# One of four block sums by adding DMAs, four of eight tile pairs in u and gate, and two loads placed anew

## The chip, the cores and the metric

The kernel runs on one core of a Trainium2 chip. The metric is device time in microseconds of one execution; the time before is the median of three runs. The engines are TensorE (PE; its weight loads are PEld), VectorE (DVE), ScalarE (ACT), GpSimd (POOL) and SyncE (SP). SP and POOL issue the DMAs, each from a queue worked in order; the chip's 16 DMA engines carry out what all queues issue.

## The reference

The model has two layers with a width of 2048 for 256 positions, all in fp32.

```python
def rms_norm(x, g): return x * rsqrt(mean(x * x) + EPS) * g
def gmlp_branch(xn, w_in, v_g, w_s, b_s, w_out):          # layer 0
    proj = xn @ w_in                                       # 2048 x (u 4096 | v 4096 | gate 4096)
    u, v = gelu(proj of u), rms_norm(gelu(proj of v), v_g)
    mixed = einsum('gts,bnsgc->bntgc', w_s * causal, v by chunks of 128 rows, 16 groups) + b_s
    return (u * mixed * silu(gate)) @ w_out                # 4096 x 2048
def stick_breaking_branch(xn, w_in, w_out):                # layer 1
    q, k, v, gate = split(xn @ w_in)                       # 2048 x 8192, 16 heads of 128
    a = where(mask, exp(log_sigmoid(z) + tail sums of log_sigmoid(-z)), 0)   # z = q k^T / sqrt(128)
    return ((a @ v) * silu(gate)) @ w_out                  # 2048 x 2048
for each layer: h = h + branch(rms_norm(h, norm_g[i]))
return rms_norm(h, final_g)
```

## The kernel before, in words

Every fp32 factor is split into a high part, rounded to a shorter float, and the rest: `hi` by a cast on ScalarE (L106), `lo` by a subtraction on VectorE (L108, `cut`). A product is then three matmuls, `hi*hi`, `hi*lo`, `lo*hi` (`terms`, L112 to L114), each of 128 x 128 stationary by 512 moving columns, into a PSUM bank. The weights are read from memory once and are the moving side.

A **pair** (class `Pair`) is two blocks of 512 output columns for both row tiles `t` of 128 positions, so it has four PSUM banks and 16 k-tiles. Part of the k-tiles is multiplied by Strassen's scheme in Winograd's form. The k-tiles are taken as 8 pairs (k, k + 8); `ks` of these go through the scheme, whose four weight blocks are `b11`, `b12` (first k half; first and second columns) and `b21`, `b22`. There are seven products instead of eight, called `p1`, `p5`, `p6`, `p2`, `p7`, `p3`, `p4` in their order here, each of `ks` k-tiles by three matmuls, two k-tiles to a cut. Four of them use sums of weight blocks, which VectorE makes in place (`minus`, L213): `b11 = b12 - b11` after `p1`, `b11 = b22 - b11` after `p5`, `b12 = b22 - b12` before `p7`, and `b11 = b11 - b21` before `p4`. The sums of the left side (`Left.sums`) are made once for a layer. All k-tiles outside the scheme go through `column(j)`, a raw tile of two k-tiles with 12 matmuls at a time. `ks` is 4 in the v pairs (3 pairs, and one more without the scheme at the start) and in layer 1 (`KS_A`, `KS_B`: 8 pairs for q and k, v, and gate), and 3 for the 8 pairs of u and gate (`KS_GU`). So 19 pairs use the scheme.

`head` makes `p1` and `p5` of a pair and is interleaved with `column(1)` of the pair before; `body` makes the rest. The block tiles `b11_0` to `b22_1` have one buffer each (`sraw`), raw tiles have three (`wraw`), cut tiles five (`wspl`). All weight loads are issued on SP in the order of the program's `load` calls as far as a list of dependences goes (`chain`, only until the first v pair); beyond that the order of each engine's instructions is set by a scheduler which simulates the program.

Around u and gate stands the **mixing** (L450 to L481): for each of 8 column blocks it loads the gain `vg` (L457, 256 KB) and the mixing matrices `ws` (L458, 128 KB) on POOL, masks `ws` there (`affine_select`, L459), splits it (`wh` on ScalarE L463, `wl` on VectorE L464), multiplies and makes `ym` (L480). Its loads stand inside `tc.issue_after(powers[0])`, where `powers[0]` is the first power of -0.5 on POOL (`n_r`, L94), which comes when the squares of all of x are summed. `issue_after` puts an order on instructions of the same engine as the given one. In layer 1 POOL also masks the attention weights `a` (L592), from which ScalarE makes `ah` (L704) for the product `O` (L711) on PE.

The opening works the first v pair's k-tiles as they arrive, beside the loads of x.

Of the kernel before, what the change touches and what calls it, by code (L numbers as in the profile page):

```python
# [8 lines left out]
F32 = mybir.dt.float32  # L9
F32R = mybir.dt.float32r  # L10
BF16 = mybir.dt.bfloat16
AF = mybir.ActivationFunctionType
ALU = mybir.AluOpType

P = 128
# [1 line left out]
CB = 512  # L17
WARM = 13
KS_A = 4
KS_GU = 3  # L20
KS_B = 4


# [1 line left out]
def trunk_kernel(ctx: ExitStack, tc: tile.TileContext, x, xt, gcols, wst, a_w_in, a_v_norm_g,  # L25
# [11 lines left out]
    nc = tc.nc  # L37
    PSUM = bass.MemoryType.PSUM
    NT, D = x.shape[1], x.shape[2]
    S = NT * P  # L40
# [6 lines left out]
    NV = W // CB  # L47
# [8 lines left out]
    sraw = ctx.enter_context(tc.tile_pool(name="sraw", bufs=1))  # L56
# [6 lines left out]
    half = const.tile([P, NT], F32, name="half")  # L63
# [17 lines left out]
    ssq = const.tile([P, NT, 3, NV], F32, name="ssq")  # L81

    def f(ap):
        return ap.bitcast(F32)

    powers = []

    def rstd(idx, nparts, n, name):
        tot = const.tile([P, NT], F32, name=f"{name}_tot")
        nc.vector.tensor_reduce(tot, ssq[:, :, idx, 0:nparts], axis=mybir.AxisListType.X, op=ALU.add)  # L90
        ms = const.tile([P, NT], F32, name=f"{name}_ms")
        nc.vector.tensor_scalar(ms, tot, 1.0 / n, EPS, op0=ALU.mult, op1=ALU.add)
        r = const.tile([P, NT], F32, name=f"{name}_r")
        powers.append(nc.gpsimd.tensor_tensor(r, ms, half, op=ALU.pow))  # L94
        return r

    def squares(h, c, layer, n):
# [18 lines left out]
    class Left:  # L116
# [9 lines left out]

        def sums(self, ks, out, name):

            full = []
            for i in range(2):  # L130
                sl = slice(i * ks, (i + 1) * ks)
                fl = sraw.tile([P, 4, S], F32, tag=f"b1{i + 1}_1", name=f"{name}_full{i}")
                nc.vector.tensor_add(fl[:, 0:ks], f(self.hi[:, sl, :]), f(self.lo[:, sl, :]))
                full.append(fl)
            a11, a12 = full[0][:, 0:ks, 0:P], full[1][:, 0:ks, 0:P]
            a21, a22 = full[0][:, 0:ks, P:S], full[1][:, 0:ks, P:S]
            sm = [sraw.tile([P, 2, 4, P], F32, tag=f"b2{i + 1}_1", name=f"{name}_sm{i}") for i in range(2)]
            s1, s2, s3, s4 = sm[0][:, 0, 0:ks], sm[0][:, 1, 0:ks], sm[1][:, 0, 0:ks], sm[1][:, 1, 0:ks]
            nc.vector.tensor_add(s1, a21, a22)
            nc.vector.tensor_sub(s3, a11, a21)  # L140
            nc.vector.tensor_sub(s2, s1, a11)
            nc.vector.tensor_sub(s4, a12, s2)
            for i, si in enumerate((s1, s2, s3, s4)):
                nc.scalar.copy(out[:, 0, i], si)
                nc.vector.tensor_sub(out[:, 1, i], si, f(out[:, 0, i]))
            self.s, self.ks = out, ks

        def sum_part(self, i, k):
# [19 lines left out]
    def ins_of(x):  # L168
        return x.ins if hasattr(x, "ins") else x
# [9 lines left out]
    class Pair:  # L179
# [31 lines left out]
        def minus(self, into, b0, b1):  # L211
            for g in range(len(self.groups)):
                nc.vector.tensor_sub(into[g], b0[g], b1[g])  # L213

        def head(self):
            left = self.left
            self.b11, self.b12 = self.load(0, 0), self.load(0, 1)
            self.a = self.bank("a")
            yield from self.block(self.b11, lambda k: left.part(k, 0), self.a, "p1", True)
            self.b22, self.b21 = self.load(1, 1), self.load(1, 0)  # L220
            self.minus(self.b11, self.b12, self.b11)
            self.e = self.bank("e")
            yield from self.block(self.b11, lambda k: left.sum_part(0, k), self.e, "p5", True)
            self.minus(self.b11, self.b22, self.b11)

        def body(self):
            left, off = self.left, self.left.ks
            b11, b12, b22, b21 = self.b11, self.b12, self.b22, self.b21

            def block(*args):  # L230
                for _ in self.block(*args):
                    pass
            a, e = self.a, self.e
            b = self.bank("b")
            nc.scalar.copy(b, a)
            es = jk.tile([P, CB], F32, tag="es", bufs=1, name=f"{self.name}_es")
            nc.scalar.copy(es, e)
            block(b11, lambda k: left.sum_part(1, k), b, "p6")
            c = self.bank("c")
            nc.scalar.copy(c, b)  # L240
            self.minus(b12, b22, b12)
            block(b21, lambda k: left.part(off + k, 0), a, "p2")
            nc.vector.tensor_add(b, b, es)
            block(b12, lambda k: left.sum_part(2, k), c, "p7")
            d = self.bank("d")
            nc.scalar.copy(d, c)
            self.minus(b11, b21, b11)
            block(b22, lambda k: left.sum_part(3, k), b, "p3")
            block(b11, lambda k: left.part(off + k, 1), d, "p4")
            nc.vector.tensor_add(c, c, es)  # L250
            self.banks = ((a, d), (b, c))
            if self.mid is not None:
                self.mid()
            for _ in self.column(0):
                pass
# [79 lines left out]
    def home(tag, shape, dtype, name):  # L335
        return big.tile(shape, dtype, tag=tag, name=name)
# [4 lines left out]
    left = Left(x_hi, x_lo)  # L341
# [24 lines left out]
    def split_x(k):  # L366
# [2 lines left out]
        nc.scalar.activation(x_hi[:, k, :], xk, AF.Identity, scale=g)  # L369
        nc.vector.scalar_tensor_tensor(x_lo[:, k, :], xk, g, f(x_hi[:, k, :]), op0=ALU.mult, op1=ALU.subtract)  # L370

    def evac_v(b, t, bank):
        vs = v[:, t, b * CB:(b + 1) * CB]
        nc.scalar.activation(vs, bank, AF.Gelu_apprx_tanh, scale=r1[:, t:t + 1])
        junk = jk.tile([P, CB], BF16, tag="junk", name=f"junkv{b}_{t}")
        nc.scalar.activation(junk, vs, AF.Square, accum_out=ssq[:, t, 1, b:b + 1])


    banks = [[ps_acc.tile([P, CB], F32, tag="acc", name=f"v0_acc{t}{j}") for t in range(NT)] for j in range(2)]
# [32 lines left out]
    for i in range(KD // 4):  # L412
# [32 lines left out]
    with ExitStack() as lg:  # L445
# [5 lines left out]
        def mixing(b):  # L451

            vg = pa.tile([P, CB], F32, tag="vg", name=f"vg{b}")
            ws = pb.tile([P, GPB, P], F32, tag="ws", name=f"ws{b}")

            with tc.issue_after(ins_of(powers[0])):
                nc.gpsimd.dma_start(vg, a_v_norm_g[0:1, b * CB:(b + 1) * CB].to_broadcast([P, CB]))  # L457
                nc.gpsimd.dma_start(ws, wst[:, b * GPB:(b + 1) * GPB, :])  # L458
            nc.gpsimd.affine_select(ws, ws, pattern=[[0, GPB], [1, P]], compare_op=ALU.is_ge, fill=0.0,  # L459
                                    base=0, channel_multiplier=-1)  # L460
            wh = pb.tile([P, GPB, P], F32R, tag="wh", name=f"wh{b}")
            wl = pb.tile([P, GPB, P], F32R, tag="wl", name=f"wl{b}")
            nc.scalar.copy(wh, ws)  # L463
            nc.vector.tensor_sub(wl, ws, f(wh))  # L464
            mixed[b] = []
            for t in range(NT):
                vh = pb.tile([P, CB], F32R, tag="vh", name=f"vh{b}_{t}")
                vl = pb.tile([P, CB], F32R, tag="vl", name=f"vl{b}_{t}")
                vs = v[:, t, b * CB:(b + 1) * CB]
                nc.scalar.activation(vh, vs, AF.Identity, scale=rv[:, t:t + 1])  # L470
                nc.vector.scalar_tensor_tensor(vl, vs, rv[:, t:t + 1], f(vh), op0=ALU.mult, op1=ALU.subtract)
                mp = ps_ms.tile([P, CB], F32, tag="ms", name=f"mix{b}_{t}")
                for j in range(GPB):
                    o = mp[:, j * GD:(j + 1) * GD]
                    sl = slice(j * GD, (j + 1) * GD)
                    nc.tensor.matmul(o, wh[:, j, :], vh[:, sl], start=True, stop=False)
                    nc.tensor.matmul(o, wh[:, j, :], vl[:, sl], start=False, stop=False)
                    nc.tensor.matmul(o, wl[:, j, :], vh[:, sl], start=False, stop=True)
                ym = pa.tile([P, CB], F32, tag=f"ym{t}", bufs=2, name=f"ym{b}_{t}")
                nc.vector.tensor_mul(ym, mp, vg)  # L480
                mixed[b].append(ym)  # L481
# [30 lines left out]
    with ExitStack() as lo_:  # L512
# [361 lines left out]
```

## Time and profile before

| what | value |
|---|---|
| median of three runs | 1179.2 us (1177.38 to 1179.94) |
| the profiled execution | 1180.04 us |
| its span, first to last instruction | 1178.3 us |
| mean granted clock of TensorE | 0.996 of full speed |
| busy: PE, VectorE, ScalarE, POOL | 1160.8, 945.5, 773.9, 47.7 us |
| DMA | 235.88 MB, mean 200 GB/s |
| its queues | q1 hardware_dynamic 229.67 MB, q0 software_dynamic 4.20 MB |

The span is what the trace covers; the execution's own time is 1.7 us longer. Stages of the span, roughly: v to 190 us, u and gate to 510, the first output projection to 720, q, k, v, gate and attention to 1080, then the last projection and the norm. A busy PE is not PE at its peak, as matmuls overlap: they start 0.23 us apart while one is shown as 0.39 us long. Idle time of another engine costs nothing by itself.

### The profile page before, as it was taken

The numbers are of one execution on the slowest core, as the hardware profiler recorded it, in microseconds if no ns is written. First come the engines' busy times: TensorE is split into PE (matmuls) and PEld (weight loads), VectorE is DVE, ScalarE is ACT, GpSimd is POOL, SyncE is SP. The second block draws the span as 40 slices with busy tenths as digits, with TensorE's granted clock in tenths as the row PEclk, the third lists the DMA queues.
The fourth block names the chain that finished last, engine by engine and source line by source line (L and its number), as shares of the span: only waits on it lengthen the run. The fifth ranks groups of instructions, "written<-read, shape, count | busy, mean of one in ns | idle before, by whom it ended". The sixth has DMA issues, their size and how long they took to land.

```text
span 1178.3 us, 14877 instructions
## 1 busy us (share of the span) xinstructions
PE 1160.8 (99%) x5393; PEld 961.4 (82%) x5393; DVE 945.5 (80%) x1050; ACT 773.9 (66%) x996; POOL 47.7 (4%) x55
## 2 busy tenths in 40 slices
PE   9899999999999999999999999999999999999997
PEld 6688888888888888888888887888888878888887
DVE  6889888998988987966556469999889989896564
ACT  7667577776766666765444456688679687885452
POOL 0210000110000000000000000002010000000000
PEclk9999999999999999999999999999999999999999
DMA  9875566576567576376556676466474564526772
GB/s 317 300 244 177 186 214 211 165 223 217 160 218 227 160 229 217 92 232 236 192 190 200 217 268 236 137 235 189 133 248 162 162 214 148 178 72 218 259 223 100
DMA packets 119609, 235.88 MB, mean 200 GB/s; under 512 B 7920, under 2 KB 12144, under 8 KB 119024
## 3 DMA queue, kind: packets, MB, share of 16 engines
q1 hardware_dynamic: 117648, 229.67, 59.8%
q0 software_dynamic: 1168, 4.20, 1.3%
q10 hardware_dynamic: 720, 1.07, 0.2%
q8 instruction: 42, 0.69, 0.2%
q14 instruction: 31, 0.25, 0.1%
HBM read 230.71 MB, written 4.19 MB: 199 GB/s over the span
## 4 chain that ended last, share of the span: by engine, by line
PE 77%; DVE 7%; ACT 6%; DMA 4%; issue 4%; POOL 0%; SPq 0%; POOLq 0%; DVEq 0%; ACTq 0%
PE o_acc L114 5%; PE o_acc L112 5%; PE o_acc L113 5%; PE gu_a L113 2%; PE gu_a L114 2%; PE gu_a L112 2%; PE gu_b L113 2%; PE gu_b L112 2%; PE gu_b L114 2%; PE f_acc L113 2%; PE f_acc L112 2%; PE f_acc L114 2%; PE gu_d L112 2%; PE gu_d L113 2%; PE gu_d L114 2%
## 5 line engine op out<-in xcount | busy, mean ns | idle before, releaser
L307 DVE TENSOR_TENSOR o_lo<-o_raw,o_hi 128x1024 fp32r<-128x1024 f32 x64 | 78.3, 1224 | 75.2 <-ACT o_hi L305 75.0
L305 ACT CAST o_hi<-o_raw 128x1024 fp32r<-128x1024 f32 x64 | 67.3, 1053 | 88.5 <-PE o_acc L114 62.4
L106 ACT CAST gu_hi<-gu_raw 128x1024 fp32r<-128x1024 f32 x80 | 82.9, 1052 | 62.8 <-DMA gu_raw<-in_a_w_in 45.6
L108 DVE TENSOR_TENSOR gu_lo<-gu_raw,gu_hi 128x1024 fp32r<-128x1024 f32 x80 | 96.3, 1217 | 30.2 <-ACT gu_hi L106 29.8
L106 ACT CAST gu_p_hi<-gu_b 128x1024 fp32r<-128x1024 f32 x112 | 91.5, 835 | 40.1 <-PE gu_c L114 22.6
L108 DVE TENSOR_TENSOR gu_p_lo<-gu_b,gu_p_hi 128x1024 fp32r<-128x1024 f32 x112 | 104.5, 954 | 4.6 <-ACT gu_p_hi L106 4.3
L112 PE MATMUL o_acc<-o_hi,yc 128*128 128x512 f32 x256 | 100.4, 392 | 0.0
L114 PE MATMUL o_acc<-o_hi,yc 128*128 128x512 f32 x256 | 99.8, 390 | 0.0
L113 PE MATMUL o_acc<-o_lo,yc 128*128 128x512 f32 x256 | 99.6, 389 | 0.0
L106 ACT CAST qk_p_hi<-qk_b 128x1024 fp32r<-128x1024 f32 x56 | 57.4, 1049 | 16.5 <-PE o_acc L114 6.9
L108 DVE TENSOR_TENSOR qk_p_lo<-qk_b,qk_p_hi 128x1024 fp32r<-128x1024 f32 x56 | 67.1, 1218 | 1.2 <-ACT qk_p_hi L106 1.0
L108 DVE TENSOR_TENSOR v_lo<-v_raw,v_hi 128x1024 fp32r<-128x1024 f32 x40 | 48.2, 1219 | 21.8 <-ACT v_hi L106 21.5
L106 ACT CAST v_hi<-v_raw 128x1024 fp32r<-128x1024 f32 x40 | 41.5, 1052 | 30.6 <-DMA v_raw<-in_a_w_in 22.4
L213 DVE TENSOR_TENSOR gu_b<-gu_b,gu_b 128x1024 f32<-128x1024 f32 (+1 forms) x64 | 60.2, 954 | 0.5
L307 DVE TENSOR_TENSOR f_lo<-f_raw,f_hi 128x1024 fp32r<-128x1024 f32 x28 | 34.2, 1224 | 30.1 <-ACT f_hi L305 29.9
L114 PEld LDWEIGHTS o_acc<-o_hi,yc 128*128 128x128 f32 x256 | 48.0, 188 | 10.0
L113 PEld LDWEIGHTS o_acc<-o_lo,yc 128*128 128x128 f32 x256 | 48.1, 188 | 9.8
L112 PEld LDWEIGHTS o_acc<-o_hi,yc 128*128 128x128 f32 x256 | 48.1, 188 | 9.7
L112 PE MATMUL f_acc<-f_hi,y_hi 128*128 128x512 f32 (+1 forms) x160 | 55.6, 347 | 0.0
L114 PE MATMUL f_acc<-f_hi,y_lo 128*128 128x512 f32 (+1 forms) x160 | 55.6, 347 | 0.0
L113 PE MATMUL f_acc<-f_lo,y_hi 128*128 128x512 f32 (+1 forms) x160 | 55.5, 347 | 0.0
L106 ACT CAST v_p_hi<-v_b 128x1024 fp32r<-128x1024 f32 x42 | 42.8, 1054 | 15.6 <-DVE v_b L213 14.4
(491 smaller groups left out, 3377.4 us busy)
## 6 DMA issues: line engine op xcount, KB each, us to landing
gu_raw<-in_a_w_in SPq DMA_DIRECT2D x64, 512.0 KB, 4.5
o_raw<-in_a_w_out SPq DMA_DIRECT2D x64, 512.0 KB, 4.4
v_raw<-in_a_w_in SPq DMA_DIRECT2D x39, 512.0 KB, 5.1
gu_b<-in_a_w_in SPq DMA_DIRECT2D x32, 512.0 KB, 4.8
qk_b<-in_b_w_in SPq DMA_DIRECT2D x32, 512.0 KB, 4.8
qk_raw<-in_b_w_in SPq DMA_DIRECT2D x32, 512.0 KB, 3.9
f_raw<-in_b_w_out SPq DMA_DIRECT2D x32, 512.0 KB, 4.2
v_b<-in_a_w_in SPq DMA_DIRECT2D x24, 512.0 KB, 5.6
```

What stands on the lines that cost most here:

```text
L106: nc.scalar.copy(hi[:, 0:n], raw[:, 0:n])
L108: nc.vector.tensor_sub(lo[:, 0:n], raw[:, 0:n], f(hi[:, 0:n]))
L112: nc.tensor.matmul(acc, lh, hi, start=first, stop=False, skip_group_check=True)
L113: nc.tensor.matmul(acc, lh, lo, start=False, stop=False, skip_group_check=True)
L114: nc.tensor.matmul(acc, ll, hi, start=False, stop=last, skip_group_check=True)
L213: nc.vector.tensor_sub(into[g], b0[g], b1[g])
L305: nc.scalar.copy(hi, raw)
L307: nc.vector.tensor_sub(lo, raw, f(hi))
```

## The change

- `KS_GU` goes from 3 to 4: a pair of u and gate has 4 of 8 tile pairs in the scheme, all its cuts and sums are 1024 wide, and a column has 4 raw tiles instead of 5.
- The sum `b12` with `b22` is no longer made on VectorE. A new function `plus` issues two DMAs on POOL, each reading 512 KB of `b22` from memory once more and adding it to `b12` in SBUF. Signs elsewhere change so that the sum is an addition: `b11 = b22 + b11` is a `tensor_add` now, and the left side's sums are mirrored.
- `b21` is loaded by the program after `p5` instead of with `b22`.
- The mixing loads stand inside `issue_after` of `norms[NV - 1]`, the last of the first pairs' squares of v (ScalarE), instead of `powers[0]` (POOL).
- `left.sums` works in pieces of four k-tiles; with 4 this is one piece as before.

```diff
-KS_GU = 3
+KS_GU = 4
...
-    powers = []
...
-        powers.append(nc.gpsimd.tensor_tensor(r, ms, half, op=ALU.pow))
+        nc.gpsimd.tensor_tensor(r, ms, half, op=ALU.pow)
...
-            nc.vector.tensor_add(s1, a21, a22)
-            nc.vector.tensor_sub(s3, a11, a21)
-            nc.vector.tensor_sub(s2, s1, a11)
+                nc.vector.tensor_sub(s1, a21, a22)
+                nc.vector.tensor_sub(s3, a21, a11)
+                nc.vector.tensor_sub(s2, a11, s1)
...
+        def plus(self, into, i, j):
+
+            for g, (k, n) in enumerate(self.groups):
+                nc.gpsimd.dma_start(into[g], self.src(i * self.left.ks + k, n, j), accum_op=ALU.add)
...
-            self.b22, self.b21 = self.load(1, 1), self.load(1, 0)
+            self.b22 = self.load(1, 1)
             self.minus(self.b11, self.b12, self.b11)
+            self.plus(self.b12, 1, 1)
             self.e = self.bank("e")
             yield from self.block(self.b11, lambda k: left.sum_part(0, k), self.e, "p5", True)
-            self.minus(self.b11, self.b22, self.b11)
+            self.b21 = self.load(1, 0)
+            for g in range(len(self.groups)):
+                nc.vector.tensor_add(self.b11[g], self.b22[g], self.b11[g])
...
             nc.scalar.copy(c, b)
-            self.minus(b12, b22, b12)
             block(b21, lambda k: left.part(off + k, 0), a, "p2")
...
-        nc.scalar.activation(junk, vs, AF.Square, accum_out=ssq[:, t, 1, b:b + 1])
+        norms.append(nc.scalar.activation(junk, vs, AF.Square, accum_out=ssq[:, t, 1, b:b + 1]))
...
-    left.sums(KS_A, home("xs", [P, 2, 4, KS_A, P], F32R, "xs0"), "s0")
+    left.sums(max(KS_A, KS_GU), home("xs", [P, 2, 4, max(KS_A, KS_GU), P], F32R, "xs0"), "s0")
...
-            with tc.issue_after(ins_of(powers[0])):
+            with tc.issue_after(ins_of(norms[NV - 1])):
```

Where the instructions stand now is shown at three places. The first is POOL's queue in the opening, before and then changed; `n_r` is the power, `vg` and `ws` the mixing's tiles.

```order
masks.py:197 MEMSET ident 128x128
masks.py:199 ISA
masks.py:199 AFFINE_SELECT ident<-ident 128x128
L94 TENSOR_TENSOR n_r<-n_ms,half 128x2
L457 DMA vg_1680<-in_a_v_norm_g 128x512
L458 DMA ws_1681<-in_wst 128x256
L458 DMA ws_2065<-in_wst 128x256
L459 AFFINE_SELECT ws_1681<-ws_1681 128x256
L459 AFFINE_SELECT ws_2065<-ws_2065 128x256
```

```order
masks.py:197 MEMSET ident 128x128
L467 DMA vg_1701<-in_a_v_norm_g 128x512
L468 DMA ws_1702<-in_wst 128x256
L468 DMA ws_2069<-in_wst 128x256
masks.py:199 ISA
masks.py:199 AFFINE_SELECT ident<-ident 128x128
L469 AFFINE_SELECT ws_1702<-ws_1702 128x256
L468 DMA ws_2436<-in_wst 128x256
L469 AFFINE_SELECT ws_2069<-ws_2069 128x256
```

The loads of `vg` and of the first two `ws` stood behind `n_r`; they stand ahead of the mask of `ident` now, and `n_r` comes after these rows.

The second is ScalarE's beginning, before and changed: the casts of the first raw tiles and of x, with its gain (`x_hi`).

```order
L369 ACTIVATE x_hi<-xr_127,cols 128x256
L106 CAST v_0_hi<-v_0_raw 128x1024
L369 ACTIVATE x_hi<-xr_127,cols 128x256 x3
L106 CAST v_1_hi<-v_1_raw 128x1024
L106 CAST v_2_hi<-v_2_raw 128x1024
```

```order
L377 ACTIVATE x_hi<-xr_127,cols 128x256
L104 CAST v_0_hi<-v_0_raw 128x1024
L473 CAST wh_1706<-ws_1702 128x256
L377 ACTIVATE x_hi<-xr_127,cols 128x256 x3
L104 CAST v_1_hi<-v_1_raw 128x1024
L104 CAST v_2_hi<-v_2_raw 128x1024
L473 CAST wh_2073<-ws_2069 128x256
```

The casts `wh` of the mixing matrices stand between the first raw tile's cast and x's tiles, and behind the third raw tile's; before, they came in the v pairs.

The third is VectorE in the head of the last pair of u and gate, before and changed. `gu_b_0` and `gu_b_1` are halves of the blocks; before, 4118 and 4120 are `b11`, 4122 and 4124 `b12`, 4181 and 4183 `b22`; in the change 4018 and 4020 are `b11`, 4022 and 4024 `b12`.

```order
L108 TENSOR_TENSOR gu_p_lo<-gu_b_0_4118,gu_p_hi 128x1024
L108 TENSOR_TENSOR gu_13_lo<-gu_13_raw,gu_13_hi 128x1024
L213 TENSOR_TENSOR gu_b_0_4118<-gu_b_0_4122,gu_b_0_4118 128x1024
L108 TENSOR_TENSOR gu_p_lo<-gu_b_1_4120,gu_p_hi 128x512
L213 TENSOR_TENSOR gu_b_0_4122<-gu_b_0_4181,gu_b_0_4122 128x1024
L213 TENSOR_TENSOR gu_b_1_4120<-gu_b_1_4124,gu_b_1_4120 128x512
L108 TENSOR_TENSOR gu_18_lo<-gu_18_raw,gu_18_hi 128x1024
L213 TENSOR_TENSOR gu_b_1_4124<-gu_b_1_4183,gu_b_1_4124 128x512
L491 SCALAR_TENSOR_TENSOR ym_0_4004<-ym_0_4004,cols,sg_0_4110 128x256 x2
```

```order
L106 TENSOR_TENSOR gu_p_lo<-gu_b_0_4018,gu_p_hi 128x1024
L106 TENSOR_TENSOR gu_18_lo<-gu_18_raw,gu_18_hi 128x1024
L214 TENSOR_TENSOR gu_b_0_4018<-gu_b_0_4022,gu_b_0_4018 128x1024
L106 TENSOR_TENSOR gu_p_lo<-gu_b_1_4020,gu_p_hi 128x1024
L214 TENSOR_TENSOR gu_b_1_4020<-gu_b_1_4024,gu_b_1_4020 128x1024
L106 TENSOR_TENSOR gu_110_lo<-gu_110_raw,gu_110_hi 128x1024
L501 SCALAR_TENSOR_TENSOR ym_0_3923<-ym_0_3923,cols,sg_0_4010 128x256 x2
L501 SCALAR_TENSOR_TENSOR ym_1_3936<-ym_1_3936,cols,sg_1_4014 128x256 x2
L106 TENSOR_TENSOR gu_p_lo<-gu_b_0_4018,gu_p_hi 128x1024
```

The two sums into 4122 and 4124 (`b12`) are gone, and the cut and sum of `b11`'s second half are 1024 wide instead of 512.

## Rows read from the trace of the kernel before

**Rows 1.** The page's first part: busy us (share of the span) xinstructions
```profile
PE 1160.8 (99%) x5393; PEld 961.4 (82%) x5393; DVE 945.5 (80%) x1050; ACT 773.9 (66%) x996; POOL 47.7 (4%) x55
```

**Rows 2.** The view of stretches: busy us (xcount) by engine, granted clock, DMA share, GB/s
```profile
8.00:28.00 20.00, 19.34 (x81) 14.77 (x82) 16.37 (x25) 16.41 (x31) 0.00 (x0) 1.00 0.99 355
...
52.00:60.00 8.00, 7.62 (x34) 5.98 (x33) 8.00 (x10) 4.95 (x7) 3.01 (x3) 1.00 0.65 196
...
190.00:510.00 320.00, 319.94 (x1465) 266.08 (x1464) 282.57 (x335) 220.83 (x276) 10.79 (x16) 1.00 0.63 196
...
720.00:1080.00 360.00, 356.72 (x1696) 296.25 (x1695) 323.00 (x352) 274.97 (x339) 19.29 (x19) 1.00 0.56 180
```

**Rows 3.** The waits of PE: waiting line, releaser, us in total, times, longest
```profile
PE v_acc L112 <- ACT v_hi L106: 2.9, 3, 2.0
...
PE qk_d L112 <- ACT qk_d L246: 1.1, 1, 1.1
PE O L711 <- ACT ah L704: 0.8, 1, 0.8
PE qk_c L113 <- DVE qk_p_lo L108: 0.6, 1, 0.6
```

**Rows 4.** The view of stretches, the end of the opening, 4 us each
```profile
44.00:48.00 4.00, 1.97 (x6) 1.08 (x5) 1.42 (x2) 2.50 (x4) 0.82 (x2) 0.82 1.04 379
48.00:52.00 4.00, 4.00 (x15) 3.27 (x15) 3.97 (x4) 4.00 (x10) 0.00 (x0) 0.75 1.05 386
```

**Rows 5.** The timeline of ScalarE: start, us, line, operation, idle before it and releaser
```profile
7.85 1.31 ACT L369 ACTIVATE x_hi<-xr,cols 128x256 fp32r<-128x256 f32 x3 [1.02 <-DMA xr<-in_xt]
...
45.50 1.04 ACT L106 CAST v_hi<-v_raw 128x1024 fp32r<-128x1024 f32 x1 [5.91 <-DMA v_raw<-in_a_w_in]
```

**Rows 6.** The timeline of PE, end of the u/gate stage
```profile
508.67 0.40 PE L112 MATMUL gu_a<-gu_hi,x_hi 128*128 128x512 f32 x1
...
510.94 0.39 PE L113 MATMUL gu_d<-gu_lo,x_hi 128*128 128x512 f32 x1
```

**Rows 7.** The view of stretches, one cycle of a u/gate pair
```profile
408.50:451.50 43.00, 43.00 (x196) 35.72 (x196) 36.60 (x43) 28.55 (x35) 0.52 (x1) 1.00 0.63 202
```

**Rows 8.** The timeline of VectorE in that cycle (sums are L213)
```profile
422.36 2.58 DVE L108 TENSOR_TENSOR gu_lo<-gu_raw,gu_hi 128x1024 fp32r<-128x1024 f32 x2 [4.37 <-ACT gu_hi L106]
...
427.14 1.22 DVE L213 TENSOR_TENSOR gu_b<-gu_b,gu_b 128x1024 f32<-128x1024 f32 x1
428.27 0.68 DVE L108 TENSOR_TENSOR gu_p_lo<-gu_b,gu_p_hi 128x512 fp32r<-128x512 f32 x1
428.87 1.82 DVE L213 TENSOR_TENSOR gu_b<-gu_b,gu_b 128x1024 f32<-128x1024 f32 x2
430.61 1.22 DVE L108 TENSOR_TENSOR gu_lo<-gu_raw,gu_hi 128x1024 fp32r<-128x1024 f32 x1
...
450.77 1.82 DVE L108 TENSOR_TENSOR gu_p_lo<-gu_b,gu_p_hi 128x1024 fp32r<-128x1024 f32 x2
```

**Rows 9.** The DMA issues: count, KB each, median us from issue to landing
```profile
vg<-in_a_v_norm_g POOLq DMA_DIRECT2D x8, 256.0 KB, 4.9
h<-in_x SPq DMA_DIRECT2D x1, 2048.0 KB, 11.3
```

**Rows 10.** The timeline of PE in the cycle of rows 7
```profile
435.34 0.39 PE L113 MATMUL gu_b<-gu_lo,x_hi 128*128 128x512 f32 x1
```

**Rows 11.** The timeline of POOL, opening and v pairs
```profile
38.02 0.72 POOL L457 DMA_DIRECT2D vg<-in_a_v_norm_g  x1
...
44.88 0.41 POOL L459 TENSOR_SCALAR_AFFINE_SELECT ws<-ws 128x256 f32<-128x256 f32 x1 [5.05 <-DMA ws<-in_wst]
...
55.37 1.10 POOL L458 DMA_DIRECT2D ws<-in_wst  x2 [9.48 <-DVE wl L464]
58.09 5.75 POOL L459 TENSOR_SCALAR_AFFINE_SELECT ws<-ws 128x256 f32<-128x256 f32 x2 [1.61 <-DMA ws<-in_wst]
```

**Rows 12.** The view of the tile ah, what its operations waited for
```profile
  POOL a L592: 8.8, 5
```

More of the change, by code (lines that the diff above doesn't have):

```diff
@@ L127, in sums @@
         def sums(self, ks, out, name):
[L129 to L138, printed above, removed]
-            nc.vector.tensor_add(s1, a21, a22)
-            nc.vector.tensor_sub(s3, a11, a21)
-            nc.vector.tensor_sub(s2, s1, a11)
[L142 to L145, printed above, removed]
+            for k0 in range(0, ks, 4):
+                n = min(4, ks - k0)
+                full = []
+                for i in range(2):
+                    sl = slice(i * ks + k0, i * ks + k0 + n)
+                    fl = sraw.tile([P, 4, S], F32, tag=f"b1{i + 1}_1", name=f"{name}_full{i}{k0}")
+                    nc.vector.tensor_add(fl[:, 0:n], f(self.hi[:, sl, :]), f(self.lo[:, sl, :]))
+                    full.append(fl)
+                a11, a12 = full[0][:, 0:n, 0:P], full[1][:, 0:n, 0:P]
+                a21, a22 = full[0][:, 0:n, P:S], full[1][:, 0:n, P:S]
+                sm = [sraw.tile([P, 2, 4, P], F32, tag=f"b2{i + 1}_1", name=f"{name}_sm{i}{k0}") for i in range(2)]
+                s1, s2, s3, s4 = sm[0][:, 0, 0:n], sm[0][:, 1, 0:n], sm[1][:, 0, 0:n], sm[1][:, 1, 0:n]
+                nc.vector.tensor_sub(s1, a21, a22)
+                nc.vector.tensor_sub(s3, a21, a11)
+                nc.vector.tensor_sub(s2, a11, s1)
+                nc.vector.tensor_sub(s4, a12, s2)
+                for i, si in enumerate((s1, s2, s3, s4)):
+                    o = out[:, :, i, k0:k0 + n]
+                    nc.scalar.copy(o[:, 0], si)
+                    nc.vector.tensor_sub(o[:, 1], si, f(o[:, 0]))
             self.s, self.ks = out, ks
@@ L370, in split_x @@
         nc.vector.scalar_tensor_tensor(x_lo[:, k, :], xk, g, f(x_hi[:, k, :]), op0=ALU.mult, op1=ALU.subtract)
+    norms = []
     def evac_v(b, t, bank):
```

## The prediction

> **What bounds the kernel now.** I began with the busy times of the page: TensorE (PE) is busy 99% of the span, VectorE 80% [rows 1]. The time can change in two ways: PE gets less to do, or one of its few idle stretches closes. To find these I cut the span into stages [rows 2]. In the u and gate stage (190 to 510 us) PE is busy 319.94 of 320 us; in the q, k, v and gate pairs of the second layer (720 to 1080) it misses 3.3 us; from 8 to 28 us it misses 0.7, at a DMA share of 0.99. The list of PE's waits says on whom [rows 3]: `v_hi` of the opening (2.9 us), `qk_d`, `O`, `qk_c`.
>
> The opening has its largest loss between 44 and 52 us: the granted clock is 0.82 and then 0.75, and PE runs 6 and 15 matmuls in 4 us each [rows 4]. The idle time comes first: ScalarE's cast of `v_18_raw`, at 45.50, waited 5.91 us for its DMA [rows 5], and PE stood 2.0 us behind it [rows 3]; the lowest clock comes after. Elsewhere a matmul follows the next in 0.2265 us (ten steps from 508.67 to 510.94 [rows 6], listed without a gap), so 8 us hold 35; 21 ran, and 14 times 0.2265 makes a loss of 3.2 us. The DMA share of 1.04 to 1.05 says that transfers set the time there, and the mixing DMAs lie in them.
>
> **The change part by part.**
>
> *Matmuls.* With 3 of 8 k-tile pairs a u/gate pair has 7 blocks of 3 x 3 matmuls and 10 remaining k-tiles of 12: 63 + 120 = 183. With 4 it is 84 + 96 = 180. Eight pairs lose 24 matmuls; at 0.2265 us [rows 6] that is **-5.4 us**. PE is the bound there, so all of it counts as long as the feed keeps up. For the feed I read one cycle, 408.5 to 451.5: VectorE is busy 36.60 of 43.00 us [rows 7]. Per pair it had 21 operations of 1024 columns and 11 of 512; it gets 28 and none. Starts lie 1.13 us apart behind one of 1024 (427.14 to 428.27) and 0.60 behind one of 512 (428.27 to 428.87) [rows 8]: +7.9 - 6.6 = +1.3 us, so 37.9 beside a PE cycle of 43.0 - 0.7 = 42.3. The cover is 4.4 us a pair. The longest wait of the cycle, 4.37 us before the last raw tiles [rows 8], remains once per column: three raw buffers held three of five tiles, now three of four. Bounds: -5.4 and 0.
>
> *The third sum.* `b12` becomes `b12 + b22` by two adding DMAs, so two operations leave VectorE in each of the 19 pairs. In the 11 pairs that had 4 tile pairs already this is pure relief, 2 x 1.13 us a pair off an engine that is busy 323 of 360 us from 720 to 1080 [rows 2]. What it is worth is the part of PE's waits that VectorE's lateness makes there: among `qk_c` 0.6, `qk_d` 1.1 and `O` 0.8 [rows 3]. Bounds: -3.3 (PE's whole idle time there) and 0; I take **-1.5**, not quite half, as two of the three name ScalarE.
>
> *The adding DMAs.* 38 of 512 KB, 19.9 MB more read. No row shows one. The nearest are POOL's own `vg` loads, 4.9 us from issue to landing; far above lies a 2 MB load, 11.3 [rows 9]. The first sum, behind which they stand, ends by 430.7 in the cycle read, and the cut of `b12` is at 450.77 on VectorE [rows 8]: some 18 us of slack, so landings of 5 or 11 us are hidden. Their traffic meets raw tiles: the one that VectorE finished at 431.83 [rows 8] is first used at 435.34 [rows 10], 3.5 us of lead. At a DMA share of 0.63 and 202 GB/s [rows 7], 8.7 MB a cycle, 1.05 MB more raises the share by 0.08 at a plain load's price, by 0.23 at three times. I take **+0.5**, close to the plain end; the other end is the second rival's.
>
> POOL works in order, so an adding DMA that waits for the first sum holds what stands behind it: the `vg` loads, `n_r` of the second layer, a mask beside the first `bg` pair. The sums are ahead of all these in VectorE's order, and an issue takes 0.55 us (1.10 for two [rows 11]). I count nothing; bound +2, inside the range.
>
> *The weight block loaded later.* Only the first v pair changes on SP: `v_112` and `v_114` move ahead of `b21`'s two loads. 1 MB leaves the place, and the adding DMAs bring 1 MB to it. Nothing.
>
> *The mixing loads.* The condition names an instruction of ScalarE while the loads stand on POOL, and the order shows what it does: nothing. `vg` and two `ws` go from behind `n_r` (38.02 us [rows 11]) to the start of POOL's queue, and their casts among ScalarE's first rows, ahead of `x_hi` of tiles 1 to 3. That is the opposite of holding them. In favour: 0.5 MB leave the stretch before `v_18_raw`. At 379 to 386 GB/s [rows 4] 512 KB take 1.37 us, so `v_18_raw` lands up to 1.4 us sooner; PE's 2.0 us shrink, and the low clock behind them may not come. Against: the same 0.5 MB and 0.25 MB of the next two `ws` enter the first 28 us, where transfers fill 0.99 of the time [rows 2]: 2.1 us. Issued in the first 3 us (0.72 for `vg` and 1.10 for two `ws` [rows 11]) and 4.9 us long like `vg` [rows 9], `ws` lands near 7.6 us, and the `x_hi` behind its cast started at 7.85 anyway [rows 5]; so the casts add a few tenths. Bounds: -3.2 (the whole loss, no delay) and +2.1; I take **-0.6**, their middle.
>
> Sum: -5.4 - 1.5 + 0.5 - 0.6 = -7.0. The profiled execution took 1180.04 us, 0.8 above the median of 1179.2; from that median the forecast is **1172.2 us**.
>
> **A rule against the change.** From 52 to 60 us VectorE was busy 8.00 of 8.00 us [rows 2]. In that time POOL took 1.10 us to issue two `ws` DMAs, 0.55 each after 0.72 for `vg` at 38.02, while two of its `affine_select`s took 5.75 us after 0.41 for one at 44.88 [rows 11]. So the trace shows POOL's operations on SBUF slowed by a busy VectorE, and its DMA issues not. The Trainium skill, SBUF — State Buffer, section "Who interferes with whom", says that a VectorE instruction with two SBUF inputs contends with GpSimd's reads, and that a DMA that VectorE seems to stall was one issued from GpSimd, short of port time to generate its descriptors. On the reads the trace agrees; on the DMAs no row shows it. The third rival is what it would do here.
>
> **The rivals.** *The feed takes the matmuls' place (0.13).* If 14 wide cuts instead of 7 wide and 7 narrow put VectorE behind PE in the first blocks of a pair's body, the u/gate cycle stays at 43.0 us. For it: the cuts lie denser there. Against: 4.4 us of cover. The 5.4 are lost: 1177.6 us.
>
> *An adding DMA costs the engines about three plain ones (0.15).* It reads memory, reads the tile and writes it. At three times 1.37 us, one ahead of a raw tile delays that by 4.1 us, against 3.5 of lead; with the tile behind it late too I put PE's wait at 1 us in each of 19 pairs: +19, less the 0.5 counted, **1190 us, slower**. It decides from 3.5 / 1.37, some 2.6 times a plain load; below that the lead absorbs it. For it: the extra read. Against: a share of 0.63 leaves 16 us of a cycle free.
>
> *POOL is kept waiting by VectorE (0.07).* If an adding DMA's issue grew by the 4 us that an `affine_select` did, two would delay a mask behind them by 8 us. `ah` waits for POOL's `a` already, 8.8 us in five [rows 12], and `O` for `ah` [rows 3]; at four such places 4 us each would reach PE: 1172.2 + 16 = 1188 us. Against: the 0.55 us issues.
>
> *The early mixing loads only cost (0.10).* The change does not do what it says there, `v_18_raw` is as late as before, and +2.1 stands in place of -0.6: 1174.9 us, or 1177 where a longer idle time at the start lowers the clock too.
>
> **How the numbers follow.** The forecast has 0.55. A measurement of this kernel can tell 0.2% (2.4 us) from no change. Faster (below 1176.8): the forecast and half of the last rival, 0.60. Same: the first rival and the other half, 0.18. Slower: the second and third, 0.22. The range runs from 1168 (all good ends together would be 1167, which I don't expect) to 1188, leaving out half of the two slow rivals and a little below. The forecast's own range is 1168 to 1176.
>
> **What would show it.** Right: 24 fewer matmuls; a u/gate cycle near 42.3 us with PE busy throughout; the software queue at about 24 MB; adding DMAs that land in 5 to 11 us; no PE wait on the cuts of `b12`; less than 2.0 us before `v_18`. Wrong: a cycle of 43 us or more, PE waits of about 1 us on raw tiles in every pair, POOL issues of several us, or a clock below 1.00 in more of the first 60 us than before.

## The result and the profile after

The change took 1169.59 us (median of 4 runs, 1168.55 to 1169.92) against 1179.57 of the kernel before on the same chip: a ratio of 0.9918, interval 0.9901 to 0.9935. It is faster by 10 us, 3 more than forecast, inside the range. The profiled execution took 1169.53 us with a span of 1167.6.

The stretches of the changed kernel, in the columns of [rows 2]:

```profile
0.00:8.00 8.00, 4.33 (x13) 1.53 (x13) 0.82 (x3) 2.00 (x3) 2.52 (x9) 1.00 0.63 173
8.00:28.00 20.00, 17.57 (x70) 14.29 (x71) 15.56 (x24) 15.28 (x28) 4.26 (x6) 0.91 0.98 353
...
40.00:52.00 12.00, 11.15 (x48) 8.55 (x47) 7.77 (x9) 5.75 (x7) 4.82 (x2) 1.00 1.05 360
52.00:60.00 8.00, 8.00 (x37) 6.60 (x37) 7.86 (x8) 6.00 (x10) 1.19 (x1) 1.00 1.08 330
...
190.00:510.00 320.00, 320.00 (x1465) 266.69 (x1464) 292.17 (x308) 229.55 (x264) 28.57 (x30) 1.00 0.74 220
...
720.00:1080.00 360.00, 359.08 (x1720) 300.44 (x1719) 309.04 (x335) 276.38 (x336) 28.40 (x31) 1.00 0.68 202
```

PE is as full from 190 to 510 as before, and from 720 to 1080 it misses 0.9 us where it missed 3.3. VectorE is busier in u and gate (292 after 283 us) and less so in layer 1 (309 after 323). In the first 8 us PE runs 13 matmuls where it ran 16 (4.33 us busy, before 6.06), and these 13 are the opening's warm-up, which needs no weights. The clock from 8 to 28 is 0.91: it is 0.86 and 0.71 in two slices of 4 us from 8 to 16 and 1.00 from 16 to 60. The kernel before had 0.82 and 0.75 from 44 to 52, so a low stretch of about the same length has moved from there to the start. Where the 10.7 us of span went is read from first and last starts of some tiles on PE (columns of the view of one tile: count, least, median and greatest ns, first to last start). For u and gate the matmul by the `lo` half is taken (`gu_p_lo`), as 698 matmuls come before its first one in each run compared below; the one before it, by `gu_p_hi`, is issued earlier or later in some. Before:

```profile
L112 PE MATMUL v_acc<-v_hi,x_hi x64: 387/389/792, 6.9 to 63.6; 128*128 128x512 f32 x64
```
```profile
L113 PE MATMUL gu_a<-gu_p_lo,x_hi x48: 389/389/396, 171.4 to 494.1; 128*128 128x512 f32 x48
```
```profile
L112 PE MATMUL qk_a<-qk_p_hi,x x32: 388/389/478, 710.6 to 952.1; 128*128 128x512 f32 x32
```
```profile
L112 PE MATMUL f_acc<-f_hi,y_hi x160: 277/389/478, 1080.9 to 1169.8; 128*128 128x512 f32 x96, 128*128 128x256 f32 x64
```

And after the change:

```profile
L110 PE MATMUL v_acc<-v_hi,x_hi x64: 387/389/628, 10.4 to 63.6; 128*128 128x512 f32 x64
```
```profile
L111 PE MATMUL gu_a<-gu_p_lo,x_hi x64: 389/389/396, 170.4 to 490.4; 128*128 128x512 f32 x64
```
```profile
L110 PE MATMUL qk_a<-qk_p_hi,x x32: 389/389/476, 703.5 to 940.4; 128*128 128x512 f32 x32
```
```profile
L110 PE MATMUL f_acc<-f_hi,y_hi x160: 278/389/478, 1070.2 to 1159.1; 128*128 128x512 f32 x96, 128*128 128x256 f32 x64
```

The first matmul comes 3.5 us later, the end of `v_acc` at the same time, `gu_a` 1.0 earlier, layer 1's first product 7.1 earlier and the last projection 10.7 earlier. So the opening and the v pairs gave 1.0 us, u, gate and the first output projection 6.1, layer 1 3.6. A second profiled execution of the changed kernel (`e9_change_again`) has `gu_a` at 168.9 instead of 170.4, so the first of these parts is known to 1.5 us only.

PE's waits, to set beside [rows 3]:

```profile
PE v_acc L110 <- ACT v_hi L104: 5.4, 2, 4.8
...
PE O L721 <- ACT ah L714: 0.8, 1, 0.8
PE v_acc L111 <- DVE v_lo L106: 0.7, 1, 0.7
PE qk_d L110 <- ACT qk_d L254: 0.4, 1, 0.4
```

`qk_c` is gone, `qk_d` fell from 1.1 to 0.4; the first weights' wait, up to 4.8 us, is new. The queues and the adding DMAs of u and gate, in the view of DMA issues (columns of [rows 9]; of a queue its packets, MB and share of the 16 engines):

```profile
q1 hardware_dynamic: 117136, 229.67, 58.8%
q0 software_dynamic: 11504, 24.12, 11.7%
...
gu_b<-in_a_w_in SPq DMA_DIRECT2D x64, 512.0 KB, 5.0
...
gu_b<-in_a_w_in POOLq DMA_DIRECT2D x16, 512.0 KB, 7.6
```

The software queue moved 24.12 MB in 11.7% of the engines' time. Against 4.20 MB and 1.3% before, that is 0.52% for a MB; the hardware queue has 58.8% for 229.67 MB, 0.26%. An adding DMA thus takes **twice** the engines' time of a plain one, and in u and gate it lands in 7.6 us in the median.

### The profile page after: what moved, and what is told of

The parts are those of the page before. It is cut to its first block, busy times and chain, and to the rows that moved or that the text cites. A ratio compares the mean times of both kernels' runs of the same rounds, so it can differ in the third digit from the quotient of the medians.

```text
span 1167.6 us, 14826 instructions
## 1 busy us (share of the span) xinstructions
PE 1150.5 (99%) x5369; PEld 957.8 (82%) x5369; DVE 929.7 (80%) x996; ACT 784.4 (67%) x980; POOL 87.9 (8%) x93
## 3 DMA queue, kind: packets, MB, share of 16 engines
q1 hardware_dynamic: 117136, 229.67, 58.8%
q0 software_dynamic: 11504, 24.12, 11.7%
## 4 chain that ended last, share of the span: by engine, by line
PE 91%; DMA 3%; ACT 2%; DVE 2%; issue 2%; SPq 0%; POOLq 0%; POOL 0%; DVEq 0%; ACTq 0%
PE o_acc L110 5%; PE o_acc L112 5%; PE o_acc L111 5%; PE gu_b L111 2%; PE gu_a L111 2%; PE gu_a L112 2%; PE gu_a L110 2%; PE gu_b L110 2%; PE gu_b L112 2%; PE f_acc L112 2%; PE f_acc L111 2%; PE f_acc L110 2%; PE gu_c L111 2%; PE gu_d L112 2%; PE gu_d L111 2%; PE gu_c L110 2%
## 5 line engine op out<-in xcount | busy, mean ns | idle before, releaser
L104 ACT CAST gu_p_hi<-gu_b 128x1024 fp32r<-128x1024 f32 x112 | 115.4, 1051 | 37.4 <-PE gu_c L112 16.8
L106 DVE TENSOR_TENSOR gu_p_lo<-gu_b,gu_p_hi 128x1024 fp32r<-128x1024 f32 x112 | 133.7, 1216 | 3.1 <-ACT gu_p_hi L104 2.7
L104 ACT CAST gu_hi<-gu_raw 128x1024 fp32r<-128x1024 f32 x64 | 66.5, 1053 | 50.9 <-DMA gu_raw<-in_a_w_in 41.0
L106 DVE TENSOR_TENSOR gu_lo<-gu_raw,gu_hi 128x1024 fp32r<-128x1024 f32 x64 | 77.2, 1220 | 27.2 <-ACT gu_hi L104 27.2
L106 DVE TENSOR_TENSOR v_p_lo<-v_b,v_p_hi 128x1024 fp32r<-128x1024 f32 x42 | 50.1, 1218 | 4.3 <-ACT v_p_hi L104 4.1
L313 ACT CAST f_hi<-f_raw 128x1024 fp32r<-128x1024 f32 x28 | 29.4, 1051 | 33.0 <-DMA f_raw<-in_b_w_out 24.0
```

The costliest lines, as they stand in the source:

```text
L104: nc.scalar.copy(hi[:, 0:n], raw[:, 0:n])
L106: nc.vector.tensor_sub(lo[:, 0:n], raw[:, 0:n], f(hi[:, 0:n]))
L313: nc.scalar.copy(hi, raw)
```

## Experiments

Every run's ratio is to the kernel before, timed beside it on the same chip. The change itself was timed again only beside the last group (the two more adding DMAs below and the two tries at the end), so for the other runs a difference from the change goes across groups; the kernel before came to between 1178.45 and 1179.57 us in them.

### Are the early mixing loads a loss?

The loads tied to POOL's first power again, all else as changed:

```diff
+    powers = []
...
-        nc.gpsimd.tensor_tensor(r, ms, half, op=ALU.pow)
+        powers.append(nc.gpsimd.tensor_tensor(r, ms, half, op=ALU.pow))
...
-            with tc.issue_after(ins_of(norms[NV - 1])):
+            with tc.issue_after(ins_of(powers[0])):
```

> The change with the mixing loads tied to POOL's first power again, as in the kernel before, all else as changed. Theory A (the early mixing loads delay the first weights: the first matmul came 3.6 us later, and only part is given back near 45 us): the first matmul is at 6.9 us again, PE waits about 2 us before v_18, and the time is 1167.5 to 1169. Theory B (the early loads are worth it, since they left the stretch before v_18): 1170.5 to 1173, with the clock below 1.00 near 48 us again.

1168.73 us (1167.65 to 1169.75), ratio 0.9916 (0.9900 to 0.9932). The first matmul is back at 6.8 us, yet the end is only 1.3 us earlier in the profiled executions and 0.9 in the medians: within what the runs scatter. The 2 us of wait before `v_18` that theory A also named did not come back. POOL issued the loads at 41.12 us, later than the kernel before (38.02), and still the cast of `v_18_raw` began at 44.14, no wait of PE for `v_hi` was longer than 0.8 us, and the clock stayed at 1.00 from 8 to 60. So it was not the early place of the loads that took away the low clock near 48 us. Then the loads were really held, behind the second v pair's adding DMAs on POOL:

```diff
...
-            with tc.issue_after(ins_of(norms[NV - 1])):
+            with tc.issue_after(ins_of(adds[3])):
```

> The change with the mixing loads held behind the last adding DMA of the second v pair on POOL, so that they really come in mid v (about 90 us). Theory A: neither the start nor the stretch before v_18 holds them; first matmul at 6.9 us, PE's wait before v_18 under 1 us, 1165.5 to 1168. Theory B (the opening is bound by the sum of its transfers, so the start's delay cost nothing that was not lost later anyway): 1169 to 1170.

1171.07 us (1168.04 to 1171.97), ratio 0.9928 (0.9911 to 0.9945). Two of its six runs lie near 1168, four near 1171; the profiled one is a 1168.04, and in it the start is back at 6.7 us and PE waits 1.2 us for VectorE in the second v pair. Why it falls into two groups the single profile doesn't show. The median lies above the ranges of both theories. Neither placement can be told from the change: of the 3.5 us at the start, 1 us or less is found at the end.

### The matmuls

```diff
-KS_GU = 4
+KS_GU = 3
```

> The change with 3 of 8 tile pairs in u and gate again. Theory A (24 matmuls at 0.2265 us, PE-bound stage): 1169.6 + 5.4 = 1175, up to 1176.5 if the whole 6.9 us by which the stage became shorter belong to it. Theory B (the stage became shorter because VectorE lost a sum): not over 1171.5.

1174.56 us (1173.44 to 1175.95), ratio 0.9964 (0.9952 to 0.9976). That is 5.0 above the change: theory A, a little under its 1175, 24 matmuls at 0.2265 us being 5.4. In the profile `gu_a` (170.8) to layer 1's first product (709.9) is 539.1 us long, after 533.1 in the change and 539.2 in the kernel before: 6.0 by this reading, and with 3 tile pairs the adding DMAs changed nothing in u and gate.

### The sum on VectorE

The adding DMAs taken out, the sum made where the kernel before made its difference, with 4 tile pairs in u and gate:

```diff
-            self.plus(self.b12, 1, 1)
...
+            for g in range(len(self.groups)):
+                nc.vector.tensor_add(b12[g], b22[g], b12[g])
             block(b21, lambda k: left.part(off + k, 0), a, "p2")
```

> The change without the adding DMAs: the sum of b12 and b22 is made on VectorE, where the kernel before made its difference. Theory A (VectorE's lateness made PE's waits in layer 1, and in u and gate VectorE then has 40 of 42.3 us): the stage of layer 1 loses some 3 us again, u and gate up to 2: 1172 to 1175. Theory B (the relief is paid for by the adding DMAs' traffic): 1169 to 1170.5. Theory C (VectorE becomes the bound in u and gate): 1177 or more.

1191.20 us (1190.72 to 1192.17), ratio 1.0107 (1.0089 to 1.0124): **slower than the kernel before**, 21.6 above the change. Theory C. Of the profile's 22.1 us, 2.1 lie ahead of `gu_a` (172.5 after 170.4), 4.0 in layer 1 (370.7 us long after 366.7) and 16.0 in u, gate and the first projection (549.1 after 533.1): 2.0 in each of the eight pairs, about the two operations at 1.13 us that VectorE got back. PE now waits there for VectorE's cuts of blocks; the lists of the kernel before and of the change have no such wait:

```profile
PE gu_a L111 <- DVE gu_p_lo L106: 3.3, 6, 0.6
PE gu_c L111 <- DVE gu_p_lo L106: 2.6, 7, 0.7
```

One cycle in it (from one cut of VectorE to the same of the next pair), and one of the change (columns of [rows 7]):

```profile
412.00:456.33 44.33, 43.31 (x192) 34.86 (x191) 39.41 (x42) 28.55 (x32) 0.54 (x1) 1.00 0.61 196
```
```profile
405.99:448.00 42.01, 42.01 (x192) 34.95 (x191) 37.23 (x39) 29.09 (x33) 2.94 (x3) 1.00 0.77 233
```

VectorE is busy 39.41 of 44.33 and 37.23 of 42.01 us, 89% in both. What fills the rest is one wait, before the fourth raw tile of the column; first the sum on VectorE, then the change:

```profile
437.71 1.23 DVE L106 TENSOR_TENSOR gu_lo<-gu_raw,gu_hi 128x1024 fp32r<-128x1024 f32 x1 [4.85 <-ACT gu_hi L104]
```
```profile
421.78 1.22 DVE L106 TENSOR_TENSOR gu_lo<-gu_raw,gu_hi 128x1024 fp32r<-128x1024 f32 x1 [4.68 <-ACT gu_hi L104]
```

39.41 + 4.85 = 44.26 of 44.33; 37.23 + 4.68 = 41.91 of 42.01. The wait begins with VectorE's own work. In the change its cut of the column's first raw tile ends at 414.8 and sets a buffer free, SP issues the fourth tile's load at 414.85, ScalarE casts it at 420.69, and VectorE goes on at 421.78. Where VectorE is late the wait is no shorter (4.85 us), so it is fixed and VectorE has no room in either: in the change PE's and VectorE's cycles are equal to 0.1 us, and two operations more lengthen it by their full time. The other half of the square, 3 tile pairs and the sum on VectorE:

```diff
-KS_GU = 4
+KS_GU = 3
```

> The change with 3 of 8 tile pairs in u and gate and the sum of b12 and b22 on VectorE: what is left of the change is the opening (mixing loads, b21). Theory A (with 3 tile pairs VectorE can make the sum, so in u and gate the adding DMA is worth nothing and its worth lies in layer 1 and the v pairs): 1177 to 1180, that is 3 to 5 over the 1174.6 with adding DMAs, and u/gate as long as in the kernel before. Theory B (VectorE was a bound in u and gate already): over 1184.

1179.46 us (1177.72 to 1180.63), ratio 1.0006 (0.9997 to 1.0015), theory A. In its profile u, gate and the first projection take 539.2 us, as in the kernel before, and layer 1 369.1, 2.4 more than with adding DMAs. So the two parts together:

| us | sum on VectorE | sum by adding DMAs |
|---|---|---|
| 3 of 8 tile pairs | 1179.46 | 1174.56 |
| 4 of 8 tile pairs | 1191.20 | 1169.59 |

Adding DMAs alone give 4.9 us in the medians (2.8 in the profiles, 2.4 of it in layer 1), the fourth tile pair with them 5.0 more, and without them it costs 11.7. The four come from three groups; their ratios to the kernel before are 1.0006 and 0.9964, 1.0107 and 0.9918, which says the same. The corner at the top left is the kernel before in all but the opening, and takes its time.

### Is an adding DMA free?

The two DMAs of a pair issued twice, one behind the other, in 15 of the 19 pairs:

```diff
             self.plus(self.b12, 1, 1)
+            if not self.name.startswith("qk"):
+                self.plus(self.b12, 1, 1)
```

> The change with the adding DMAs issued twice, one behind the other, in the v, u/gate, v-projection and last-gate pairs (15 of 19; not q and k), so b12 gets b22 two times and the result is another: 30 adding DMAs and 15.7 MB more. Theory A (time and traffic of an adding DMA are hidden; landing is 7.6 us in the change and the slack about 18 us, so two in a row still end in time): within 1.5 us of the change, 1168.5 to 1171. Theory B (an adding DMA takes about twice the engine time of a plain one, so doubling it makes raw tiles late, as in the second rival): 0.5 to 1 us a pair, 1177 to 1185. Theory C (two in a row end after the cut of b12 is due): 2 us a pair or more, 1200.

1210.75 us (1209.66 to 1219.22), ratio 1.0287 (1.0259 to 1.0314), 41 above the change. ScalarE's timeline at the cut of `b12` in one u/gate pair shows on what:

```profile
395.21 1.05 ACT L104 CAST gu_p_hi<-gu_b 128x1024 fp32r<-128x1024 f32 x1
404.09 1.04 ACT L104 CAST gu_p_hi<-gu_b 128x1024 fp32r<-128x1024 f32 x1 [7.83 <-DMA gu_b<-in_a_w_in]
```

The second half's cast waits 7.83 us for the adding DMA. In 9 of the 15 doubled pairs that cast begins 0.1 us after the last landing: two DMAs behind two others don't fit there. ScalarE's waits before these nine casts come to 45 us. In the change the same cast waits for nothing, and between landing and cast remain 3.8 us in the first q and k pair, 5.1 in the first v pair and 7 to 15 in the others (last landing by issue and duration of each of the 19, against the cast's start). Theory C, at 2.7 us for each doubled pair (a share of it is the mean clock, 0.979). To take traffic apart from this wait, two more adding DMAs were put behind the pair's own in u and gate, into tiles that nothing reads, 768 KB a pair:

```diff
-                nc.gpsimd.dma_start(into[g], self.src(i * self.left.ks + k, n, j), accum_op=ALU.add)
+                self.added = nc.gpsimd.dma_start(into[g], self.src(i * self.left.ks + k, n, j), accum_op=ALU.add)
...
+            for s_, k, n in zip(spare, (0, 2), (2, 1)):
+                with tc.issue_after(ins_of(self.added)):
+                    nc.gpsimd.dma_start(s_, self.src(left.ks + k, n, 1), accum_op=ALU.add)
...
```

> The change with two more adding DMAs in each u/gate pair, 512 and 256 KB into tiles that nothing reads, issued behind the pair's own two: traffic without anything that waits for it, 768 KB in each of 8 pairs. Theory A (the 41 us of the doubled DMAs were the wait of b12's cut alone, traffic is hidden): not over 1 us above the change, DMA share in u/gate up by some 0.09. Theory B (traffic of adding DMAs, at twice a plain one's engine time, makes raw tiles late): 0.5 us or more a pair, 4 to 10 us above the change, with PE waits on gu_hi or gu_lo.

1170.91 us (1168.49 to 1172.77), ratio 0.9937 (0.9921 to 0.9953), 0.9 above the change beside it, with overlapping runs. From 190 to 510 us:

```profile
190.00:510.00 320.00, 319.92 (x1462) 266.12 (x1461) 291.45 (x307) 227.94 (x264) 43.15 (x44) 1.00 0.84 237
```

The DMA share went from 0.74 to 0.84, about the 0.85 of the doubled run, and PE has 319.92 of 320 us. Theory A: traffic of this size is hidden, and what counts is whether the last adding DMA lands before its cut. The opposite test, the second sum as adding DMAs too, where the next cut stands close behind:

```diff
-            for g in range(len(self.groups)):
-                nc.vector.tensor_add(self.b11[g], self.b22[g], self.b11[g])
+            self.plus(self.b11, 1, 1)
```

> The change with the second sum, b11 = b22 + b11 between p5 and p6, made by adding DMAs as well: 1.05 MB and two DMAs more a pair, two operations of 1.2 us fewer on VectorE. Theory A (an adding DMA is free only where its landing of 7 to 8 us fits into slack; here b11 is cut some 5 us behind, with 4 us of lead): PE waits 1.5 to 5 us a pair for p6's cuts, 1195 to 1265. Theory B (relief of VectorE counts more): 1165 to 1170.

1285.25 us in a single execution, 116 above the change, 6.1 a pair and above theory A's range. PE's waits now lead with `p6`, whose cut it is (`gu_b`, `v_b`), and ScalarE's casts for it stand behind the landings; one pair of u and gate:

```profile
PE gu_b L110 <- ACT gu_p_hi L104: 13.4, 13, 1.8
PE gu_b L111 <- DVE gu_p_lo L106: 10.3, 16, 0.8
PE v_b L110 <- ACT v_p_hi L104: 7.8, 4, 3.7
```
```profile
408.98 1.05 ACT L104 CAST gu_p_hi<-gu_b 128x1024 fp32r<-128x1024 f32 x1 [7.55 <-DMA gu_b<-in_a_w_in]
412.94 1.99 ACT L104 CAST gu_p_hi<-gu_b 128x1024 fp32r<-128x1024 f32 x2 [2.92 <-DMA gu_b<-in_a_w_in]
```

In all 19 pairs both casts begin 0.1 us after the landing of an adding DMA. The waits listed on PE don't add up to 116 us; the mean granted clock was 0.970, which takes a share.

### The late weight block

```diff
-            self.b22 = self.load(1, 1)
+            self.b22, self.b21 = self.load(1, 1), self.load(1, 0)
```

> The change with b21 loaded together with b22 again. Theory A (it moves only two loads of the first v pair, in whose place adding DMAs now come): 1169 to 1170.5. Theory B (it kept 1 MB out of the saturated stretch near 50 us): 1171 to 1172.5, with PE waiting 1 us or more on v_112 or v_114.

1173.04 us (1171.79 to 1175.22), ratio 0.9954 (0.9941 to 0.9967): 3 above the change. Theory B, half a microsecond over its range. ScalarE's casts of `v_112` and `v_114`:

```profile
56.50 1.04 ACT L104 CAST v_hi<-v_raw 128x1024 fp32r<-128x1024 f32 x1 [3.93 <-DMA v_raw<-in_a_w_in]
...
60.17 1.05 ACT L104 CAST v_hi<-v_raw 128x1024 fp32r<-128x1024 f32 x1 [1.68 <-DMA v_raw<-in_a_w_in]
```

They wait 3.93 and 1.68 us for their DMAs. PE has 6.11 of 8 us from 52 to 60, where the change has 8.00. Against the change's second set of runs (below) the intervals touch, so the 3 us are the medians' difference. The trace shows a delay at this place, not all of it: of the 2.4 us between the two profiled executions 1.1 lie ahead of `gu_a` (171.5 after 170.4) and the rest behind it.

### Two tries at a better opening

From 40 to 60 us the DMA share is 1.05 to 1.08 in the change, while VectorE is busy 7.8 of 12 us from 40 to 52. So the first v pair's sum went to VectorE (the first two parts of the edit), then the mixing loads were held as well (the last part); the change was timed beside both.

```diff
...
-            self.plus(self.b12, 1, 1)
+            if self.name != "v2":
+                self.plus(self.b12, 1, 1)
...
+            if self.name == "v2":
+                for g in range(len(self.groups)):
+                    nc.vector.tensor_add(b12[g], b22[g], b12[g])
             block(b21, lambda k: left.part(off + k, 0), a, "p2")
...
-            with tc.issue_after(ins_of(norms[NV - 1])):
+            with tc.issue_after(ins_of(adds[1])):
```

> The changed kernel itself, beside the three others of this group on the same chip: 1169 to 1170.5. It is the yardstick for them.

> The change with the first v pair's sum on VectorE, the other 18 pairs by adding DMAs. Theory A (from 40 to 60 us transfers are the bound and VectorE has time to spare, so there the adding DMAs are paid for): 1 to 3 us less than the change, DMA share near 50 to 60 us below 1.0. Theory B (the opening's delay has its cause before 40 us): within 0.5 us of the change.

> The same with the mixing loads held behind the second v pair's adding DMAs. Theory A (the start's 3.6 us are partly lost for good): 1 to 2 us less again, 1165 to 1168, below both kernels. Theory B (what is gained at the start is lost near 90 us, where the held loads and casts then come): no less than the run before it.

1169.99 us for the change (1169.09 to 1172.63; ratio 0.9932, 0.9917 to 0.9948), 1171.14 (1168.65 to 1174.52; 0.9946, 0.9929 to 0.9964) and 1170.02 (1168.97 to 1173.03; 0.9936, 0.9919 to 0.9953). In the first try the share from 52 to 60 fell from 1.08 to 0.67 as meant, in the second the first matmul came at 6.7 us instead of 10.7; neither moved the end. Theory A misses in both: no version that is clear of the change was found.

## Why the prediction was right, point by point

**Matmuls: right.** Forecast -5.4; with 3 tile pairs the change loses 5.0 of it again. From one pair's first adding DMA to the next the u/gate cycle is 42.2 and then 42.0 us (342.77, 384.93, 426.94), forecast 42.3. The cover behind it was not right: I put 37.9 us of VectorE beside 42.3 and called 4.4 us cover, and in the same paragraph left the wait of 4.37 us standing. The two are the same time. VectorE had nothing left, as the sum on VectorE shows at 2.0 us a pair. The first rival was thus 0.1 us of cover away from being right, and that the 5.4 came whole was luck by that much.

**The third sum: mis-sized.** I took -1.5 of at most -3.3, as two of three waits named ScalarE. Layer 1 became 3.6 us shorter in the change and 4.0 longer again with the sum back on VectorE (2.4 with 3 tile pairs in u and gate): so the sum's place decides it, also at `qk_d`, where the rows name ScalarE's copy. `O` kept its 0.8. PE's idle time in layer 1 fell by 1.9 us, its listed waits by as much; where the other 1.7 came from no row shows. The other thing missed is the term that this sum has in u and gate: as the change had the relief from the start, my sum never priced it, though without it the fourth tile pair costs 12 us.

**The adding DMAs: right in kind.** Slack of 18 us, landing in 7.6, hidden; +0.5 for traffic was about nothing. The price of twice a plain load lies under the 2.6 from which the second rival would have decided, and its mechanism, late raw tiles, did not show when 768 KB more were added to each pair. The slack is smaller than it looks: each DMA waits for its half of the first sum, and 7 to 9 us of u/gate's remain.

**POOL behind VectorE: not so.** An adding DMA takes POOL 1.2 us to issue, twice a `ws` load and not the 0.55 counted, in stretches with VectorE nine tenths busy. The first, issued at 46.38 while VectorE stood still (45.81 to 48.38), took 1.27, so VectorE is not what makes it 1.2. The Trainium skill's rule (SBUF — State Buffer, "Who interferes with whom") of a DMA from GpSimd short of port time does not show as a wait here: the 38 issues take 1.16 to 1.34 us. The same section counts `tensor_tensor`, which is nearly all that VectorE runs here, among the operations that did not stall a DMA, and with that the trace agrees; the third rival had read the rule too widely. `n_r`, an operation with inputs in SBUF, took 6.23 us at 37.32, where the rule's other half fits.

**The late block: wrong.** I priced it at nothing since adding DMAs bring back the 1 MB that it takes away. But an adding DMA waits for the first sum (the first is issued at 46.38 us), where `b21`'s loads waited for nothing, so `v_112` and `v_114` got ahead of both: loading `b21` early again costs some 3 us in the medians.

**The opening: the sum fits, its parts don't.** Forecast -0.6 between -3.2 and +2.1; opening and v pairs gave -1.0, and -2.3 with the loads back behind the power (`gu_a` at 169.1), so not for the reason forecast: that it fits is luck. The condition holds nothing, as said. But the loads cost more at the start than the 2.1 us bound: the first `ws` is masked at 10.02 us, where I had it landed near 7.6, the first cast waits 5.51 us, and the first matmul comes 3.5 us late.

```profile
9.33 1.04 ACT L104 CAST v_hi<-v_raw 128x1024 fp32r<-128x1024 f32 x1 [5.51 <-DMA v_raw<-in_a_w_in]
...
47.30 1.05 ACT L104 CAST v_hi<-v_raw 128x1024 fp32r<-128x1024 f32 x1 [6.10 <-DMA v_raw<-in_a_w_in]
```

I had counted on the casts behind `x_hi` and not on the first weights, which are loaded beside the mixing loads. PE stands 4.8 us, and the clock of 0.91 from 8 to 28 us comes behind that idle stretch; with the first matmul at 6.8 us it was 1.00 there. One of the signs named for being wrong, a clock below 1.00 in more of the first 60 us than before, is on the edge: the low stretch is as long as before in this profile and longer in the second one of the change (0.56 and 0.59 from 8 to 16 us). Against it, `v_18_raw` is cast at 47.30, 1.8 us later than before, where PE has come later too and waits 0.6 instead of 2.0; the clock stays at 1.00 there. All four placements tried end within 1.5 us of the change, about what the start of `gu_a` differs by between its own two profiled executions. That agrees with an opening that is bound by its transfers as a whole, but does not show it.

What stays open: whether the mixing loads' place is worth one microsecond, why the held loads gave two groups of runs, and what took away the low clock near 48 us, or whether the kernel before has it in every execution (the mean clocks of its executions are 0.995 to 0.999, that of the profiled one 0.996).

## What to carry to other kernels

An engine's free time in a cycle is no cover if a fixed wait takes it: add busy time and the waits that would stay, and compare that with the cycle. A transfer that does arithmetic is as good as free where it lands well before its reader, whatever it costs the engines while they have room (here up to a share of 0.84), and a stall where it doesn't; measure the distance from landing to reader, and double the transfer to see how far the edge is. Two changes can be worth 5 us and minus 12 each alone and 10 together, as here, so test them as a square.

## What the runs showed of the hardware

An accumulating DMA from memory into SBUF took about twice the engine time per byte of a plain load (0.52% against 0.26% of the span's engine time for a MB), 7.6 us in the median from issue to landing for 512 KB where plain loads of that size took 5.0, and 1.2 us of POOL's queue where a `ws` load took 0.55. A tensor operation on POOL of 128 x 2 elements took 6.23 us beside a busy VectorE and 0.72 at 190.03, where VectorE stood still.
